# Attention scores on halves of TensorE's rows, in one layer of a hybrid encoder

## The chip, the cores and the metric

The kernel is one program on one core of a Trainium2 chip. The metric is the device time of one execution in microseconds, lower is better. The core has five engines that run their own instruction streams: TensorE (PE, with its weight loads shown apart as PEld), VectorE (DVE), ScalarE (ACT), GpSimd (POOL) and SyncE (SP), whose queue here does nothing but start transfers.

## What is computed

The layer normalises 1024 tokens and 16 meta tokens of width 1024, multiplies them by one wide input matrix, and feeds two branches: a neighbourhood attention over a token grid 64 wide and 16 high, and a gated linear recurrence in both directions. Both are gated, added, projected back, and followed by a feed-forward block with squared ReLU and a last norm. The change is in the attention branch:

```python
q_na, k_na, v_na = ...            # 8 heads of 64, for 16 meta and 1024 grid tokens
s_win  = einsum('brchd,brjwhd->bhrcjw', qg, k_blk) * scale   # 8 rows of keys for each query
s_win  = where(in_win, s_win + bias, -1e30)                  # window 16 wide in columns
s_meta = einsum('brchd,bmhd->bhrcm', qg, km) * scale
p      = softmax(concatenate([s_win, s_meta]))
o_grid = p_win @ v_blk + p_meta @ vm
```

All inputs and outputs are float32. The kernel keeps that accuracy by splitting a float32 number into a high part in TensorE's faster type (fp32r) and a low part, the remainder, and by adding three products: high by high, high by low, low by high.

## The kernel before, in words

The attention runs between the recurrence and the gates. The grid is cut into 8 strips of 8 columns by 16 rows, so a strip is 128 tokens, one tile of 128 partitions. A query in strip s sees keys in strips s-1, s and s+1 and the 16 meta keys; each strip of keys has 128 + 16 columns (SW = 144), so scores are 432 wide, or 288 in the first and the last strip. Two heads of 64 make a pair, there are four pairs (line 547), and each pair does this:

- It projects queries, keys and values (`proj`, lines 564, 582, 590): 24 matmuls for every 512 tokens, through the lines 135 to 137. What leaves PSUM is split into high and low by ACT and DVE. Queries go to `QX`, one tile per head: 64 partitions hold the high part, the other 64 the low part. Keys go to `KS`, the high part twice, and to `KL`, the low part in 64 partitions and zeros in the other 64. That takes four ACT and two DVE instructions for a piece of keys, two and two for a piece of queries (lines 558 to 581).
- `scores(s, i)` for strip s and head i (lines 605 to 623): two matmuls over all 128 rows, QX by KS (high times high plus low times high) and QX by KL (high times low), into one PSUM bank `nsc`, of which there are two. DVE adds the bias and takes the minimum (line 618; the signs are turned), ACT takes the exponential and the sum (620), DVE scales by the reciprocal (621, 622).
- `values(s, i)` (lines 625 to 663): three or four transposes of the probabilities on TensorE (633, 635) into `ppt`, the split into the tiles `PT` (ACT 644, DVE 645), and after each fourth strip the products with the values (649 to 658) into `pov`, added up by DVE (660, 662).

Heads are taken one after the other for four strips each (line 665), scores run two steps ahead of values, and `PT` has one pair of buffers, laid out by distance of key strip and query strip.

The order of instructions on each engine is made by a scheduler when the program is built, and each engine then keeps it. It fills TensorE with the next pair's projections while a pair's softmax runs, and in the last pair with the first products of the gates (`first_gates`, line 715, through the lines 691 to 693). These need the weight blocks that SP loads (line 123) and ACT and DVE split (125, 126). The gates also need four operands made by POOL during the attention (lines 228 to 246), which `second_operand` (739 to 745) loads again into the tile `gv`, of which there are five, and splits.

## Time and profile before

| | us |
|---|---|
| median of three runs | 1549.21 |
| lowest and highest run | 1549.18, 1552.02 |
| the profiled execution | 1550.2 |
| its span on the core | 1548.4 |
| TensorE busy in the span | 1502.1 |
| VectorE busy | 1008.4 |
| ScalarE busy | 654.7 |

A row of a timeline gives the start, the duration, the engine, the source line, what it writes and reads, its shape, and in brackets the idle time of the engine before it with what ended that. TensorE's matmuls follow each other before the one ahead has come to its end, so what one costs is read from the distance of two starts, not from its duration. Where a row stands for several instructions (x2) its start is that of the first.

### The profile page before, as it was taken

To read this page: it belongs to the slowest core of one execution; us is meant where nothing else is said; L and a number is where in the kernel's file an instruction comes from. 1 tells how busy PE (TensorE), PEld (TensorE's weight loads), DVE (VectorE), ACT (ScalarE), POOL (GpSimd) and SP (SyncE) were. 2 spreads that over 40 slices of the span, in tenths; PEclk is the share of its full clock that TensorE was granted. 3 is DMA by queue.
4 is the path that set the end of the run, shared out by engine and by line. 5 is a ranking of instruction groups with operands and counts; after the bars stand their busy time and mean duration, and the time that the engine had idled before them with its cause. 6 is when DMAs were issued, how large, how long until landed. Compare 5 with 4: busy or idle time off the path is not lost.

```text
span 1548.4 us, 23448 instructions
## 1 busy us (share of the span) xinstructions
PE 1502.1 (97%) x9188; PEld 1253.5 (81%) x9188; DVE 1008.4 (65%) x1592; ACT 654.7 (42%) x1168; POOL 401.8 (26%) x359
## 2 busy tenths in 40 slices
PE   6999999999999998999999999999999999999998
PEld 5788888878888887888888887888888788887886
DVE  6666666664876877666475369666666444879566
ACT  6231313124665666334122245555555433434444
POOL 4413131315315310011000032444444200237033
PEclk9999999999999999999999999999999999999999
DMA  5101010113123128434951324444444576563224
GB/s 181 43 28 56 28 56 28 55 29 128 49 72 119 55 69 272 136 123 163 339 178 41 109 91 148 165 155 153 153 150 148 169 273 233 190 231 107 98 82 150
DMA packets 142335, 195.61 MB, mean 126 GB/s; under 512 B 8064, under 2 KB 90112, under 8 KB 142224
## 3 DMA queue, kind: packets, MB, share of 16 engines
q1 hardware_dynamic: 133856, 173.40, 33.8%
q10 hardware_dynamic: 6192, 13.37, 2.2%
q0 software_dynamic: 2176, 7.34, 1.3%
q8 instruction: 72, 1.18, 0.3%
q14 instruction: 39, 0.32, 0.1%
HBM read 139.55 MB, written 54.53 MB: 125 GB/s over the span
## 4 chain that ended last, share of the span: by engine, by line
PE 83%; DVE 9%; issue 3%; ACT 2%; DMA 2%; POOL 1%; DVEq 0%; POOLq 0%; SPq 0%; ACTq 0%
PE mm L135 11%; PE mm L136 10%; PE mm L137 10%; PE mm L1112 4%; PE pa L1112 4%; PE pb L691 4%; PE pb L692 4%; PE pb L693 4%; PE pc L1112 4%; PE pb L1112 4%; PE pc L693 2%; PE pc L692 2%; PE pc L691 2%; PE pa L692 2%; PE pa L691 2%
## 5 line engine op out<-in xcount | busy, mean ns | idle before, releaser
L135 PE MATMUL mm<-aT,hi 128*128 128x512 f32 (+2 forms) x640 | 230.2, 360 | 2.7 <-DVE QX L563 1.5
L137 PE MATMUL mm<-aT,lo 128*128 128x512 f32 (+2 forms) x640 | 227.8, 356 | 0.0
L136 PE MATMUL mm<-aT,hi 128*128 128x512 f32 (+2 forms) x640 | 226.6, 354 | 0.0
L97 DVE TENSOR_TENSOR dl<-ur,dh 128x1024 fp32r<-128x1024 f32 x55 | 76.6, 1393 | 93.7 <-ACT dh L96 93.5
L135 PEld LDWEIGHTS mm<-aT,hi 128*128 128x128 f32 x640 | 121.9, 191 | 17.2 <-issue 1.7
L137 PEld LDWEIGHTS mm<-aT,lo 128*128 128x128 f32 x640 | 121.8, 190 | 13.5 <-POOL lo L126 0.3
L136 PEld LDWEIGHTS mm<-aT,hi 128*128 128x128 f32 x640 | 121.9, 190 | 12.4
L96 ACT CAST dh<-ur 128x1024 fp32r<-128x1024 f32 x55 | 57.9, 1053 | 162.5 <-issue 78.1
L125 ACT CAST hi<-raw 128x1024 fp32r<-128x1024 f32 x36 | 37.8, 1051 | 106.7 <-PE mm L136 75.6
L974 ACT CAST wh<-sx 128x512 fp32r<-128x512 f32 x70 | 42.5, 618 | 94.7 <-DMA sx<-in_w_up 33.1
L975 DVE TENSOR_TENSOR wl<-sx,wh 128x512 fp32r<-128x512 f32 x70 | 51.2, 738 | 31.0 <-ACT wh L974 31.0
L975 DVE TENSOR_TENSOR wl<-raw,wh 128x512 fp32r<-128x512 f32 x46 | 50.2, 1090 | 23.7 <-ACT wh L974 22.9
L979 ACT ACTIVATE uv<-uv 128x512 f32<-128x512 f32 x48 | 30.4, 632 | 67.4 <-DVE uv L1090 50.0
L1095 POOL TENSOR_TENSOR us<-u,uv 128x512 f32<-128x512 f32 x15 | 24.0, 1603 | 133.4 <-ACT uv L980 133.4
L1202 POOL TENSOR_TENSOR w<-w,tt 128x512 f32<-128x512 f32 x16 | 23.3, 1458 | 134.0 <-DVE tt L1201 120.4
L399 POOL TENSOR_TENSOR Y<-X,TN 128x512 f32<-128x512 f32 x20 | 35.0, 1749 | 86.1 <-DVE X L396 86.1
L691 PE MATMUL pb<-nt,wh 128*128 128x512 f32 x128 | 50.4, 394 | 3.6 <-DVE uv L1083 2.6
L126 DVE TENSOR_TENSOR lo<-raw,hi 128x1024 fp32r<-128x1024 f32 x34 | 43.2, 1270 | 15.6 <-ACT hi L125 15.4
L92 POOL TENSOR_SCALAR rtm<-ssq 128x1 f32<-128x1 f32 (+1 forms) x17 | 6.4, 376 | 180.4 <-ACT junk L924 156.0
L618 DVE CUSTOM_DVE_ANT_0 pr<-nsc,NB 128x432 f32<-128x432 f32 (+1 forms) x64 | 35.2, 559 | 26.6 <-PE nsc L613 26.5
L1112 PE MATMUL mm<-dl,dh 128*128 128x512 f32 x126 | 49.9, 396 | 2.1 <-DVE dl L97 2.1
L135 PE MATMUL mm<-o,hi 128*128 128x512 f32 x128 | 50.0, 390 | 0.6 <-DVE mix L850 0.6
(380 smaller groups left out, 4409.3 us busy)
## 6 DMA issues: line engine op xcount, KB each, us to landing
raw<-in_w_in SPq DMA_DIRECT2D x56, 512.0 KB, 3.9
ur<-usp SPq DMA_DIRECT2D x55, 512.0 KB, 3.5
raw<-in_w_up SPq DMA_DIRECT2D x16, 1024.0 KB, 5.5
usp<-us SPq DMA_DIRECT2D x60, 256.0 KB, 2.0
sg<-gsp SPq DMA_DIRECT2D x16, 512.0 KB, 4.3
w<-in_w_dn SPq DMA_DIRECT2D x16, 512.0 KB, 4.5
usp<-uv SPq DMA_DIRECT2D x30, 256.0 KB, 2.2
gsp<-gv ACTq DMA_DIRECT2D x24, 256.0 KB, 2.4
```

Of the source, the lines that this page charges most:

```text
L96: act.copy(hi, src)
L97: dve.tensor_tensor(lo, src, hi.bitcast(F32), op=ALU.subtract)
L126: eng.tensor_tensor(lo[:, :kc], raw[:, :kc], hi[:, :kc].bitcast(F32), op=ALU.subtract)
L135: pe.matmul(ps, lh, rh, start=first, stop=False)
L136: pe.matmul(ps, lh, rl, start=False, stop=False)
L137: pe.matmul(ps, ll, rh, start=False, stop=last)
L691: pe.matmul(ps, lhs[0][:, c], rhs[0][:, k], start=first and k == 0, stop=False, skip_group_check=True)
L692: pe.matmul(ps, lhs[0][:, c], rhs[1][:, k], start=False, stop=False, skip_group_check=True)
L693: pe.matmul(ps, lhs[1][:, c], rhs[0][:, k], start=False, stop=k == 3, skip_group_check=True)
L974: act.copy(v(hi), src)
L975: dve.tensor_tensor(v(lo), src, v(hi).bitcast(F32), op=ALU.subtract)
L1112: pe.matmul(ps, a[n == 2][:, q, j * P:(j + 1) * P], b[n == 1][:, q], start=first and n == 0, stop=last and n == 2, skip_group_check=True)
```

## The change

It touches four things.

1. Queries and keys are split into tiles of their own, `QH`, `QL`, `KH`, `KL`, with the two heads in the two halves of the partitions, by one ACT and one DVE instruction for each piece of both heads. The zeros in `KL` go.
2. `scores(s)` does both heads of a strip. Each head's 64 rows of TensorE are a tile of their own (`tile_position`), and three products of 64 rows (high by high, low by high, high by low) take the place of two of 128. The two heads' scores stand in the two banks of one PSUM tile, of which there is one where there were two of one bank.
3. Heads alternate within a strip, scores run one strip ahead, and the split probabilities lie four blocks to a query strip, in a pair of buffers for each head; the products with the values read them with a stride of three blocks.
4. The operands of the gates are loaded straight into the low tile and split in place; the results of the gates get five buffers of their own, in another pool.

The core of the diff ("..." for lines left out):

```diff
-    psum_pools(mx=1, s=2, t=2, b=1)
+    psum_pools(mx=1, s=1, t=2, b=1)
...
-        QX = [npl.tile([P, 8, P], F32R, name=f"QX{i}") for i in range(2)]
-        KS = [npl.tile([P, 8, SW], F32R, name=f"KS{i}") for i in range(2)]
-        KL = [npl.tile([P, 8, SW], F32R, name=f"KL{i}") for i in range(2)]
+        QH, QL = (npl.tile([P, 8, P], F32R, name=f"Q{v}") for v in "HL")
+        KH, KL = (npl.tile([P, 8, SW], F32R, name=f"K{v}") for v in "HL")
...
+        def ev_split(hi, lo):
+            def ev(ps, t0, n):
+                split(strips(hi, t0, n), strips(lo, t0, n), grid(ps))
+            return ev
...
-            def ev_q(ps, t0, n):
-                for i in range(2):
-                    b = 64 * i
-                    hi = strips(QX[i], b, t0, n)
-                    act.copy(hi, grid(ps, b))
-                    dve.tensor_tensor(strips(QX[i], 64 - b, t0, n), grid(ps, b), hi.bitcast(F32), op=ALU.subtract)
-            proj(C_QN + p * P, ev_q)
...
+            proj(C_QN + p * P, ev_split(QH, QL))
...
+            proj(C_KN + p * P, ev_split(KH, KL), mev_k)
...
-                sc = bank("s", "nsc").rearrange("p a b -> p (a b)")
-                ksl = KS[i][:, js[0]:js[-1] + 1].rearrange("p s c -> p (s c)")
-                kll = KL[i][:, js[0]:js[-1] + 1].rearrange("p s c -> p (s c)")
-                pe.matmul(sc[:, :w], QX[i][:, s], ksl, start=True, stop=False)
-                pe.matmul(sc[:, :w], QX[i][:, s], kll, start=False, stop=True)
+                sc = banks["s"].tile([P, 2, TH], F32, tag="s", name="nsc")
+                scs = [sc[:, i, :w] for i in range(2)]
+                for n, (q, k) in enumerate(((QH, KH), (QL, KH), (QH, KL))):
+                    for i in range(2):
+                        r = slice(64 * i, 64 * i + 64)
+                        pe.matmul(scs[i], q[r, s], k[r, js[0]:js[-1] + 1].rearrange("p s c -> p (s c)"),
+                                  start=n == 0, stop=n == 2, tile_position=(64 * i, 0))
...
-                    po[i] = [npr.tile([P, 22, P], F32R, tag=f"PT{q}", name=f"PT{q}") for q in range(2)]
...
-                        b = 3 * a + e0 + 3
-                        pe.matmul(ov[:, e0:e0 + ne], V[:, j, i], PH[:, b:b + ne], start=False, stop=False)
+                        b = slice(3 * e0 + a + 1, 3 * (e0 + ne - 1) + a + 2, 3)
+                        pe.matmul(ov[:, e0:e0 + ne], V[:, j, i], PH[:, b], start=False, stop=False)
...
-            steps = [(4 * g + e, i) for g in range(2) for i in range(2) for e in range(4)]
...
+            for s in [*range(8), None]:
+                if s is not None:
+                    if s % 4 == 0:
+                        PT = [[npr.tile([P, 16, P], F32R, tag=f"PT{i}{q}", name=f"PT{i}{q}") for q in range(2)]
+                              for i in range(2)]
+                    pend.append((s, *scores(s), PT))
+                if len(pend) > 1 or s is None:
+                    s_, js, prs, pts = pend.pop(0)
+                    for i in range(2):
+                        values(s_, i, js, prs[i], pts[i])
...
-            t = g_tile("gv", TH, bufs=5)
...
-            sp.dma_start(t, tsp[v][k])
-            split(aV[v][0][:, k], aV[v][1][:, k], t)
+            hi, lo = (t[:, k] for t in aV[v])
+            sp.dma_start(lo.bitcast(F32), tsp[v][k])
+            split(hi, lo, lo.bitcast(F32))
```

What the scheduler makes of it shows in the order of the instructions. On PE, where the first pair's attention begins, there stood before (nsc is the bank of scores, mm a projection, vpt the transposed values):

```order
L612 MATMUL nsc<-KS_3940,QX_3938 128x288
L613 MATMUL nsc<-KL_3942,QX_3938 128x288
L612 MATMUL nsc<-KS_3940,QX_3938 128x432
L613 MATMUL nsc<-KL_3942,QX_3938 128x432
L135 MATMUL mm<-aT_90,hi 128x512
L136 MATMUL mm<-aT_91,hi 128x512
L612 MATMUL nsc<-KS_3940,QX_3938 128x432
L613 MATMUL nsc<-KL_3942,QX_3938 128x432
```

At the same place there stands now:

```order
L595 MATMUL nsc<-KH,QH 128x288 x2
L595 MATMUL nsc<-KH,QL 128x288 x2
L595 MATMUL nsc<-KL,QH 128x288 x2
L135 MATMUL mm<-aT_90,hi 128x512
L136 MATMUL mm<-aT_91,hi 128x512
L137 MATMUL mm<-aT_90,lo 128x512
L576 MATMUL vpt<-ident,vT 128x128 x8
```

Six products of 64 rows for both heads of a strip stand where two strips of one head had two of 128 rows each. Further on in the same pair one such six is cut in two by products with the values (ppt are transposed probabilities, pov the products with the values):

```order
L617 MATMUL ppt<-ident,pr 128x128 x2
L619 MATMUL ppt<-ident,pr 128x128
L595 MATMUL nsc<-KH,QH 128x432 x2
L636 MATMUL pov<-PT_4228,Vn 64x384
L635 MATMUL pov<-PT_4227,Vn 128x256
L636 MATMUL pov<-PT_4228,Vn 64x256
L635 MATMUL pov<-PT_4227,Vn 128x128
L636 MATMUL pov<-PT_4228,Vn 64x128
L637 MATMUL pov<-PT_4228,Vn 128x512
L595 MATMUL nsc<-KH,QL 128x432 x2
L595 MATMUL nsc<-KL,QH 128x432 x2
```

This happens once in each pair, so the 32 strips make 36 unbroken runs of score products. On SP, where the last pair's attention runs, the loads of the gates' operands (from tsp) stood among the weight blocks (raw) like this:

```order
L123 DMA raw<-in_w_in 128x8x128
L765 DMA raw<-in_w_in 128x8x128
L744 DMA gv<-tsp_t_0_370 128x512
L744 DMA gv<-tsp_t_1_371 128x512
L744 DMA gv<-tsp_t_2_372 128x512
L744 DMA gv<-tsp_t_3_373 128x512
L744 DMA gv<-tsp_t_0_366 128x512
L123 DMA raw<-in_w_in 128x8x128
```

Now the first four, into aT, stand further ahead, and the second operand's go into the tile at:

```order
L726 DMA aT_93<-tsp_t_3_373 128x512
L123 DMA raw<-in_w_in 128x8x128
L747 DMA raw<-in_w_in 128x8x128 x3
L123 DMA raw<-in_w_in 128x8x128 x2
L726 DMA at_6887<-tsp_t_0_366 128x512
L726 DMA at_6887<-tsp_t_1_367 128x512
L726 DMA at_6887<-tsp_t_2_368 128x512
L123 DMA raw<-in_w_in 128x8x128
```

The tile at lies in the memory of the attention's right-hand pool, so its loads start when the last pair's attention has let go of it, and the last weight blocks of the first gates stand behind them.

More of the change, by code (lines that the diff above doesn't have):

```diff
@@ L525, in layer, with strips, grid @@
     gfp = gfs.enter_context(tc.tile_pool(name="gfp", bufs=1, side="right", reuse_waits="tile"))
-    psum_pools(mx=1, s=2, t=2, b=1)
+    psum_pools(mx=1, s=1, t=2, b=1)
     with (tc.tile_pool(name="npr", bufs=1, side="right", reuse_waits="tile") as npr,
           tc.tile_pool(name="np", bufs=1, reuse_waits="tile") as npl):
-        QX = [npl.tile([P, 8, P], F32R, name=f"QX{i}") for i in range(2)]
-        KS = [npl.tile([P, 8, SW], F32R, name=f"KS{i}") for i in range(2)]
-        KL = [npl.tile([P, 8, SW], F32R, name=f"KL{i}") for i in range(2)]
+        QH, QL = (npl.tile([P, 8, P], F32R, name=f"Q{v}") for v in "HL")
+        KH, KL = (npl.tile([P, 8, SW], F32R, name=f"K{v}") for v in "HL")
         vT = npl.tile([P, 9, P], F32, name="vT")
         V = npr.tile([P, 9, 2, P], F32R, name="Vn")
-        pool.memset(KL[0][64:128].bitcast(F32), 0.0)
-        pool.memset(KL[1][0:64].bitcast(F32), 0.0)
         pool.memset(vT[:, 8], 0.0)
-        def strips(t, p0, t0, n, w=None):
-            a = t[p0:p0 + 64, 0:8, t0 // 8:(t0 + n) // 8]
-            return a.rearrange("p s (r c) -> p s r c", c=8)
-        def grid(ps, p0):
-            return ps[p0:p0 + 64].rearrange("p (r s c) -> p s r c", s=8, c=8)
+        def strips(t, t0, n):
+            return t[:, 0:8, t0 // 8:(t0 + n) // 8].rearrange("p s (r c) -> p s r c", c=8)
+        def grid(ps):
+            return ps.rearrange("p (r s c) -> p s r c", s=8, c=8)
+        def ev_split(hi, lo):
+            def ev(ps, t0, n):
+                split(strips(hi, t0, n), strips(lo, t0, n), grid(ps))
+            return ev
         for p in range(NPAIR):
@@ L556, in layer @@
                                        op=ALU.subtract)
-            def ev_q(ps, t0, n):
-                for i in range(2):
-                    b = 64 * i
-                    hi = strips(QX[i], b, t0, n)
-                    act.copy(hi, grid(ps, b))
-                    dve.tensor_tensor(strips(QX[i], 64 - b, t0, n), grid(ps, b), hi.bitcast(F32), op=ALU.subtract)
-            proj(C_QN + p * P, ev_q)
-            def ev_k(ps, t0, n):
-                for i in range(2):
-                    b = 64 * i
-                    hi = strips(KS[i], b, t0, n)
-                    act.copy(hi, grid(ps, b))
-                    act.copy(strips(KS[i], 64 - b, t0, n), grid(ps, b))
-                    dve.tensor_tensor(strips(KL[i], b, t0, n), grid(ps, b), hi.bitcast(F32), op=ALU.subtract)
-            def mev_k(ps):
-                for i in range(2):
-                    b = 64 * i
-                    m = ps[b:b + 64].unsqueeze(1).broadcast_to([64, 8, NM])
-                    hi = KS[i][b:b + 64, :, P:]
-                    act.copy(hi, m)
-                    act.copy(KS[i][64 - b:128 - b, :, P:], m)
-                    dve.tensor_tensor(KL[i][b:b + 64, :, P:], m, hi.bitcast(F32), op=ALU.subtract)
-            proj(C_KN + p * P, ev_k, mev_k)
+            proj(C_QN + p * P, ev_split(QH, QL))
+            def mev_k(ps):
+                split(KH[:, :, P:], KL[:, :, P:], ps.unsqueeze(1).broadcast_to([P, 8, NM]))
+            proj(C_KN + p * P, ev_split(KH, KL), mev_k)
             def ev_vn(ps, t0, n):
-                for i in range(2):
-                    act.copy(strips(vT, 64 * i, t0, n), grid(ps, 64 * i))
+                act.copy(strips(vT, t0, n), grid(ps))
             def mev_vn(ps):
@@ L600, in layer, with scores @@
             block_sums(p, lambda: npl.tile([P, TH], F32, tag="bs", name="rt", bufs=3))
-            po = {}
             OT = npr.tile([P, T], F32, tag="OT", name="OT")
-            def scores(s, i):
+            def scores(s):
                 js = [j for j in (s - 1, s, s + 1) if 0 <= j < 8]
@@ L608, in scores @@
                 o = 432 if s == 0 else 720 if s == 7 else 0
-                sc = bank("s", "nsc").rearrange("p a b -> p (a b)")
-                ksl = KS[i][:, js[0]:js[-1] + 1].rearrange("p s c -> p (s c)")
-                kll = KL[i][:, js[0]:js[-1] + 1].rearrange("p s c -> p (s c)")
-                pe.matmul(sc[:, :w], QX[i][:, s], ksl, start=True, stop=False)
-                pe.matmul(sc[:, :w], QX[i][:, s], kll, start=False, stop=True)
-                pr = npr.tile([P, 432], F32, tag="pr", name="pr", bufs=5)
@@ L615, in scores @@
-                mn = npr.tile([P, 1], F32, tag="mn", name="mn", bufs=4)
-                sm = npr.tile([P, 1], F32, tag="sm", name="sm", bufs=4)
-                rc = npr.tile([P, 1], F32, tag="rc", name="rc", bufs=4)
-                dve.tensor_tensor_reduce(out=pr[:, :w], in0=sc[:, :w], in1=NB[:, i, o:o + w], scale=1.0,
-                                         scalar=3.0e38, op0=ALU.add, op1=ALU.min, accum_out=mn)
-                act.activation(pr[:, :w], pr[:, :w], AF.Exp, bias=mn, scale=-1.0, accum_out=sm)
@@ L621, in scores @@
-                dve.reciprocal(rc, sm)
-                dve.tensor_scalar(pr[:, :w], pr[:, :w], rc, None, op0=ALU.mult)
-                return js, pr
-            def values(s, i, js, pr):
+                sc = banks["s"].tile([P, 2, TH], F32, tag="s", name="nsc")
[5 more added lines that the diff above has]
+                                  start=n == 0, stop=n == 2, tile_position=(64 * i, 0))
@@ new lines, in scores @@
+                prs = []
+                for i in range(2):
+                    pr = npr.tile([P, 432], F32, tag="pr", name="pr", bufs=6)
+                    mn = npr.tile([P, 1], F32, tag="mn", name="mn", bufs=4)
+                    sm = npr.tile([P, 1], F32, tag="sm", name="sm", bufs=4)
+                    rc = npr.tile([P, 1], F32, tag="rc", name="rc", bufs=4)
+                    dve.tensor_tensor_reduce(out=pr[:, :w], in0=scs[i], in1=NB[:, i, o:o + w], scale=1.0,
+                                             scalar=3.0e38, op0=ALU.add, op1=ALU.min, accum_out=mn)
+                    act.activation(pr[:, :w], pr[:, :w], AF.Exp, bias=mn, scale=-1.0, accum_out=sm)
+                    dve.reciprocal(rc, sm)
+                    dve.tensor_scalar(pr[:, :w], pr[:, :w], rc, None, op0=ALU.mult)
+                    prs.append(pr)
@@ L626, in values @@
+                return js, prs
+            def values(s, i, js, pr, PT):
                 g, e = divmod(s, 4)
-                if e == 0:
-                    po[i] = [npr.tile([P, 22, P], F32R, tag=f"PT{q}", name=f"PT{q}") for q in range(2)]
-                PH, PL = po[i]
+                PH, PL = PT
                 m = len(js)
@@ L635, in values @@
                 pe.transpose(pt[:, m], pr[:, cen * SW + NM:cen * SW + NM + P], ident)
-                b0 = 3 * (js[0] - 4 * g) + e + 3
-                if s < 7:
-                    runs = [(0, m + 1, b0)]
-                else:
-                    runs = [(0, m, b0), (m, 1, 4 * e + 9)]
-                for k, n, b in runs:
-                    hi = PH[:, b:b + 3 * n - 2:3]
-                    act.copy(hi, pt[:, k:k + n])
-                    dve.tensor_tensor(PL[:, b:b + 3 * n - 2:3], pt[:, k:k + n], hi.bitcast(F32), op=ALU.subtract)
+                k0 = 4 * e + js[0] - s + 1
+                for k, n, b in [(0, m + 1, k0)] if s < 7 else [(0, m, k0), (m, 1, 4 * e + 3)]:
+                    split(PH[:, b:b + n], PL[:, b:b + n], pt[:, k:k + n])
                 if e < 3:
@@ L648, in values @@
                 ov = bank("b", "pov")
-                pe.matmul(ov, V[:, 8, i], PH[:, 9:22:4], start=True, stop=False)
+                pe.matmul(ov, V[:, 8, i], PH[:, 3::4], start=True, stop=False)
                 for a in range(-1, 5):
@@ L654, in values @@
                         e0, ne = es[0], len(es)
-                        b = 3 * a + e0 + 3
-                        pe.matmul(ov[:, e0:e0 + ne], V[:, j, i], PH[:, b:b + ne], start=False, stop=False)
-                        pe.matmul(ov[:64, e0:e0 + ne], V[:, j, i, :64], PL[:, b:b + ne], start=False, stop=False)
-                pe.matmul(ov, V[:, 8, i], PL[:, 9:22:4], start=False, stop=True)
+                        b = slice(3 * e0 + a + 1, 3 * (e0 + ne - 1) + a + 2, 3)
+                        pe.matmul(ov[:, e0:e0 + ne], V[:, j, i], PH[:, b], start=False, stop=False)
+                        pe.matmul(ov[:64, e0:e0 + ne], V[:, j, i, :64], PL[:, b], start=False, stop=False)
+                pe.matmul(ov, V[:, 8, i], PL[:, 3::4], start=False, stop=True)
                 low = npr.tile([64, 4, P], F32, tag="low", name="low")
@@ L663, in values @@
                                   low.rearrange("p s (r c) -> p s r c", c=8), op=ALU.add)
-            steps = [(4 * g + e, i) for g in range(2) for i in range(2) for e in range(4)]
             pend = []
-            for st in steps:
-                pend.append((*st, *scores(*st)))
-                if len(pend) > 2:
-                    values(*pend.pop(0))
-            for st in pend:
-                values(*st)
+            for s in [*range(8), None]:
[6 more added lines that the diff above has]
+                    s_, js, prs, pts = pend.pop(0)
+                    for i in range(2):
+                        values(s_, i, js, prs[i], pts[i])
             pool.dma_start(osp[1][p], OT)
@@ L782, in gate_pair @@
         chain(pb, W["s2"], aV["t2"], True)
-        u1, u3, u2 = (g_tile("gv", TH, bufs=5) for _ in range(3))
+        u1, u3, u2 = (gpr.tile([P, TH], F32, tag="gu", name="gu", bufs=5) for _ in range(3))
         dve.tensor_tensor(u1, pb, g1[m], op=ALU.add)
```

## The prediction

> **What bounds the kernel now.** I read the busy time of the engines on the page first, then the table of engines by stretches of the attention, then TensorE's waits in it. The page's first rows give the engine:

> ```profile
> PE 1502.1 (97%) x9188; PEld 1253.5 (81%) x9188; DVE 1008.4 (65%) x1592; ACT 654.7 (42%) x1168; POOL 401.8 (26%) x359
> ```

> The stretches give each engine's busy time in 20 us (PE, PEld, DVE, ACT, POOL, then granted clock, DMA share, GB/s):

> ```profile
> 440.00:460.00 20.00, 19.97 (x122) 16.82 (x122) 19.03 (x58) 14.62 (x38) 0.00 (x0) 1.00 0.10 27
> ...
> 580.00:600.00 20.00, 17.57 (x92) 14.29 (x91) 16.39 (x31) 14.91 (x29) 0.54 (x1) 1.00 0.77 249
> 600.00:620.00 20.00, 18.01 (x78) 14.31 (x77) 11.72 (x16) 12.58 (x22) 0.00 (x0) 1.00 0.86 277
> ```

> TensorE is full inside the attention (19.97 of 20) at a granted clock of 1.00, and loses time only at its end. VectorE stands close behind it (19.03). What TensorE waited for between 355 and 625 us (total, times, longest):

> ```profile
> PE ppt L633 <- DVE PT L645: 2.4, 1, 2.4
> PE mm L135 <- DVE QX L563: 1.5, 1, 1.5
> PE mm L691 <- ACT hi L125: 1.5, 1, 1.5
> PE ppt L633 <- DVE pr L622: 1.4, 3, 0.5
> PE mm L135 <- DVE KL L572: 1.2, 2, 0.6
> PE mm L693 <- DVE lo L126: 0.5, 1, 0.5
> ```

> That is 8.5 us in all. So a saving on ACT or DVE can bring 8.5 us at the very most, and the change is otherwise worth what it is worth on TensorE's own stream.

> **The change part by part.** *The score products.* The tile view counts them (durations in ns, min/median/max):

> ```profile
> L612 PE MATMUL nsc<-KS,QX x64: 292/379/469, 381.2 to 578.0; 128*128 128x432 f32 x48, 128*128 128x288 f32 x16
> L613 PE MATMUL nsc<-KL,QX x64: 291/356/366, 381.3 to 578.1; 128*128 128x432 f32 x48, 128*128 128x288 f32 x16
> ```

> The durations overlap, so the price is the distance of starts:

> ```profile
> 442.46 0.37 PE L612 MATMUL nsc<-KS,QX 128*128 128x432 f32 x1
> 442.46 0.19 PEld L613 LDWEIGHTS nsc<-KL,QX 128*128 128x128 f32 x1
> 442.66 0.35 PE L613 MATMUL nsc<-KL,QX 128*128 128x432 f32 x1
> 442.85 0.40 PE L136 MATMUL mm<-aT,hi 128*128 128x512 f32 x1
> ...
> 578.01 0.29 PE L612 MATMUL nsc<-KS,QX 128*128 128x288 f32 x1
> 578.14 0.30 PE L613 MATMUL nsc<-KL,QX 128*128 128x288 f32 x1
> 578.28 0.39 PE L692 MATMUL mm<-aT,hi 128*128 128x512 f32 x1
> ```

> A 432-wide product takes 0.195 us of the stream (442.46 to 442.85 for two), a 288-wide one 0.135 (578.01 to 578.28 for two). Now: 96 x 0.195 + 32 x 0.135 = 23.0 us. After: 24 strips of three pairs of 432 and 8 of three pairs of 288. If a pair, one product in each half of the rows, runs in the time of one: 72 x 0.195 + 24 x 0.135 = 17.3 us, so **-5.8** (before rounding). That halves of the array run side by side is seen here for halves of the columns only, in line 390:

> ```profile
> 96.49 1.15 PE L390 MATMUL sc<-QQ,X 128*64 128x64 f32 x32
> 97.57 0.50 PE L135 MATMUL mm<-aT,hi 128*128 128x512 f32 x1
> ```

> From the first of the 32 to the next line's product are 97.57 - 96.49 = 1.08 us, 34 ns each with all of the switching, where a full product of 128 columns takes 0.11 us (next fence), so an estimated 55 ns for half its width. I take rows to do the same; the case that they don't is a rival.

> *Going in and out of the tiles.* The program has one place with products on part of the rows, line 446 (16 rows), among full ones; the first row is the tile's own (ns), the rest its timeline:

> ```profile
> L462 PE MATMUL pu<-V,KT x112: 270/275/377, 111.3 to 342.3; 128*128 128x128 f32 x112
> ...
> 188.27 0.48 PE L135 MATMUL mm<-aT,hi 128*128 128x512 f32 x1
> 188.68 0.48 PE L446 MATMUL pum<-Vm,kmT 16*128 16x128 f32 x2
> 189.09 0.49 PE L462 MATMUL pu<-V,KT 128*128 128x128 f32 x2
> 189.34 0.48 PE L136 MATMUL mm<-aT,hi 128*128 128x512 f32 x1
> 189.66 0.38 PE L462 MATMUL pu<-V,KT 128*128 128x128 f32 x2
> 189.79 0.47 PE L137 MATMUL mm<-aT,lo 128*128 128x512 f32 x1
> ```

> Two of line 462 last 0.38 from the first's start to the second's end (189.66) where one lasts 0.275: 0.11 apart. The same neighbours without line 446 are the comparison. From the 512-wide product to line 446 it is 0.41, to line 462 0.32: +0.09 for going in. Line 446's two, as wide, take 0.41 to the next start, at 0.11 each 0.22: +0.19. The two of line 462 behind it take 0.25, the later two 0.13: +0.11 for having come out. Together 0.39 us for one run of row tiles. I charge it to each of the 36 unbroken runs that the order gives: **+14.0**. Some 0.09 of it may be a load that the longer products here hide, so the lower end is 36 x 0.30 = 10.8; the lowest, nothing, is a rival, because narrowing the columns costs nothing:

> ```profile
> 448.97 0.28 PE L656 MATMUL pov<-PT,Vn 128*128 128x256 f32 x1
> 449.08 0.28 PE L657 MATMUL pov<-PT,Vn 128*64 128x256 f32 x1
> 449.20 0.34 PE L656 MATMUL pov<-PT,Vn 128*128 128x384 f32 x1
> ```

> Here 0.11 to 0.12 is what 256 columns stream in either shape. I take the 0.39 since line 446 is the only one that, as the scores will, changes the rows. [...]

> *The splits.* Between 340 and 640 us:

> ```profile
> L562 ACT CAST QX<-mm 64x512 fp32r<-64x512 f32 x16 | 9.2, 580 | 1.6 <-DVE QX L563 1.0 <-PE pov L658 0.3 <-PE pov L657 0.2
> L563 DVE TENSOR_TENSOR QX<-mm,QX 64x512 fp32r<-64x512 f32 x16 | 10.9, 688 | 0.8 <-ACT QX L562 0.3
> L571 ACT CAST KS<-mm 64x512 fp32r<-64x512 f32 x8 | 4.6, 581 | 0.1
> ```

> An instruction on 64 partitions is taken to cost what one on 128 does. A piece of queries then falls from two ACT and two DVE instructions to one and one, a piece of keys from four and two to one and one. Where nothing else is queued, the projection's bank comes free 0.69 us earlier for queries (0.58 + 2 x 0.69 against 0.58 + 0.69) and 1.2 for keys (second high part after the copy: 3 x 0.58 + 0.69 = 2.4 against 1.3). Of the waits above that takes 0.7 of the 1.5 for QX and the whole 1.2 for KL: **-1.9**. All else that ACT and DVE save lies beside a full TensorE and counts nothing; the two memsets on POOL and the strided reads of the probabilities (the meta products already read with a stride of four blocks) I put at nothing, with POOL idle in the first row above as their cover.

> *Order of heads, buffers, gates.* Line 633 waits 1.4 for pr; scores run one strip ahead instead of two steps, the same distance, and TensorE comes 0.39 later each time by the switches, so I count 1.2 saved. The 2.4 for PT is the last pair's tail; now products of the gates stand between those transposes: 1.5 saved. Loading into the tile frees five buffers early, but the second operand's loads must wait for the attention's memory and stand ahead of weight blocks. Seven loads of 0.26 MB and two blocks of 0.52 are 2.9 MB, at the 277 GB/s of the last stretch 10.4 us. By the order, 82 products of the gates (144 columns add 0.06 above, so 512 take 0.228) run between the last product with values and the first that needs the last of these blocks, 18.7 us: hidden. If that cover were gone, 10 us would show. Ahead of the last product with values stand 62 of the gates' products where there were 72, so ten more are left to cover the 2.0 of hi and lo: half of that, 1.0, saved. Together **-3.7**; at the lower end nothing.

> Sum: -5.8 + 14.0 - 1.9 - 3.7 = **+2.6 us**. The profiled execution took 1550.2, 1.0 above the median of 1549.2; from it the sum gives 1552.8, and against the median **1551.8**. Its own bounds: -5.8 + 10.8 - 8.5 = -3.5, and -5.8 + 14.0 - 1.9 = +6.3.

> **The rivals.**

> *Row halves cost no switch* (lines 656 and 657 are the rule, and line 446 is slow for its 16 rows). Then -5.8 - 1.9 = -7.7 at best. But VectorE has 0.97 us of air in 20, so some comes back as its wait; with half of 5.8 given back, -4.8: 1544.4. Against it: line 446 behaves so at all four places where it stands.

> *The halves run one after the other.* 144 x 0.195 + 48 x 0.135 = 34.6 us, +11.6 in place of -5.8: 11.6 + 14.0 - 5.6 = +20.0: 1569.2. For it: no row of before shows two row tiles at once. Against it: line 390.

> *The single score tile makes TensorE wait* (the other side). Before, one bank was free for each score; now a tile holds both heads and there is one, so a strip's products start only after both of the last strip's reductions:

> ```profile
> L618 DVE CUSTOM_DVE_ANT_0 pr<-nsc,NB 128x432 f32<-128x432 f32 (+1 forms) x64 | 35.2, 559 | 26.6 <-PE nsc L613 26.5
> ```

> Two take 1.1 us, in a VectorE queue that is nearly full. The scheduler puts projections and values between strips; where these run short TensorE stands. If half of one reduction, 0.28 us, shows in all 28 later strips, it is 7.8, in half of them 3.9: +6.5 to +10.4, in the middle 1557.7. It decides if VectorE lies more than the work between two strips behind. Against it: VectorE has half of line 563's 10.9 us less to do over the attention.

> *Loads aren't hidden.* In each run two of the three load pairs would stand open, 0.10 each as in line 446: 36 x 0.20 = +7.2, so +9.8: 1559.0. Against it: 442.46, where line 613's load starts with line 612's product on the same 128 rows. [...]

> **How the numbers follow.** Chances: the forecast 0.60, free switches 0.15, halves in turn 0.08, the single tile 0.13, open loads 0.04. The measurement tells 0.2%, 3.1 us, from no change. Within the forecast's own range (1545.7 to 1555.5) I give 0.05 to faster by more than that, 0.35 to within, 0.20 to slower. Free switches add 0.15 to faster; the other three add 0.25 to slower. So 0.20, 0.35, 0.45. The range takes in the free switches with all kept, 1549.2 - 7.7 = 1541.5, and the single tile's upper end, 1559.6, and leaves out the halves in turn and the forecast's tails: 1541 to 1560.

> **What would show it.** In the changed kernel's timeline: line 595's two heads start a few ns apart and pairs 0.195 apart (if 0.39, halves run in turn); the start before a run and behind it lie some 0.2 further apart than streaming says (if not, switches are free); load rows of the second pair start with the first pair's products (if after, loads are open). Among the waits, the one for QX halves and the one for KL is gone; a new one of line 595 for the reduction means the single tile. The forecast is wrong if TensorE's idle time in the attention grows, or the runs cost under 0.2 or over 0.5 us each.

## The result and the profile after

| | before | after |
|---|---|---|
| median | 1549.20 us (4 runs, 1548.41 to 1552.02) | 1559.87 us (4 runs, 1559.21 to 1561.03) |
| profiled execution, span | 1548.4 | 1557.4 |
| ratio | | 1.0066, 95% interval 1.0049 to 1.0084 |

The changed kernel is slower by 0.66%, 10 us (7.6 to 13 by the interval). Nearly all of it lies in one stage. The next fences give it for both kernels, from the recurrence's last transposes (line 495) to the last product of the first gates (line 693, now 675): length, then busy time of PE, PEld, DVE, ACT, POOL, granted clock, DMA share, GB/s. Before:

```profile
353.17:623.42 270.25, 261.53 (x1526) 222.25 (x1524) 194.59 (x464) 167.50 (x375) 77.96 (x78) 1.00 0.34 109
```

After:

```profile
352.45:631.42 278.97, 270.75 (x1589) 217.62 (x1588) 180.19 (x440) 138.40 (x307) 73.81 (x76) 0.99 0.33 105
```

The stage is 8.7 us longer, of 9.0 between the two spans. VectorE lost 14 us of work and ScalarE 29, and it brought nothing: TensorE is the engine that is busy. This stage is what the experiments are read by below, since the whole varies (the kernel before had medians of 1549.2 to 1551.4 beside the different experiments). Each length is that of one execution, and it holds that execution's stretches of half clock on TensorE, which last 3.41 us each (last section) and cost up to half of that, 1.7 us. The kernel before had none in its stage, the changed kernel two in a row. The run zero_rows, whose TensorE does the same work in the same order in this stage, had three and took 280.7 us instead of 279.0. So differences under 2 us between two stages show nothing unless their clock is looked at.

TensorE's waits between 355 and 632 us in the changed kernel (total, times, longest):

```profile
PE ppt L617 <- DVE PT L97: 3.0, 5, 2.0
PE pov L628 <- ACT PT L96: 1.5, 1, 1.5
PE mm L673 <- ACT hi L125: 1.2, 1, 1.2
PE vpt L576 <- ACT vT L567: 0.8, 1, 0.8
PE mm L675 <- DVE lo L126: 0.5, 1, 0.5
PE ppt L617 <- DVE pr L607: 0.4, 2, 0.2
PE ppt L617 <- DVE rc L606: 0.3, 2, 0.2
```

The waits for the split queries and keys are gone, and line 595 does not appear: TensorE waits in no place for the single tile of scores. But the sum is 7.7 us where it was 8.5. The last run of score products, in the timeline:

```profile
580.81 0.39 PE L673 MATMUL mm<-aT,hi 128*128 128x512 f32 x1
581.12 0.40 PE L595 MATMUL nsc<-KH,QH 64*128 64x288 f32 x2
581.36 0.29 PE L595 MATMUL nsc<-KH,QL 64*128 64x288 f32 x2
581.49 0.29 PE L595 MATMUL nsc<-KL,QH 64*128 64x288 f32 x2
581.71 0.50 PE L674 MATMUL mm<-aT,hi 128*128 128x512 f32 x1
582.05 0.39 PE L675 MATMUL mm<-aT,lo 128*128 128x512 f32 x1
```

Each row of line 595 holds both heads, and pairs follow each other at 0.13 us, so the halves run side by side. Going in costs 0.31 - 0.23 = 0.08, the second pair comes 0.24 after the first instead of 0.135 (+0.105), going out is 0.22 (+0.085), and the next product is late by 0.34 - 0.23 = 0.11: 0.38 us for the run, where 0.39 was forecast. By the same count the other 288-wide runs between 512-wide products lie at 0.38 to 0.39.

The last pair's tail is the new part. TensorE there:

```profile
585.02 0.39 PE L675 MATMUL mm<-aT,lo 128*128 128x512 f32 x1
587.45 0.44 PE L617 MATMUL ppt<-ident,pr 128*128 128x128 f32 x2 [2.04 <-DVE PT L97]
...
590.13 0.80 PE L628 MATMUL pov<-PT,Vn 128*128 128x512 f32 x1 [1.53 <-ACT PT L96]
...
593.60 0.63 PE L673 MATMUL mm<-aT,hi 128*128 128x512 f32 x1
...
596.15 0.40 PE L675 MATMUL mm<-aT,lo 128*128 128x512 f32 x1
```

The clock that it was granted (third column from the right):

```profile
585.00:590.00 5.00, 1.51 (x8) 0.62 (x6) 4.07 (x10) 4.75 (x12) 0.00 (x0) 0.93 0.48 157
590.00:595.00 5.00, 4.87 (x16) 4.20 (x17) 4.00 (x8) 3.18 (x5) 0.00 (x0) 0.50 0.53 164
```

TensorE was busy for 1.5 us of the first 5, and its granted clock was 0.50 from 589.30 to 596.13. The twelve products with the values took 593.60 - 590.13 = 3.47 us; before, the first head's same twelve took 1.92, by these two rows (the first of them, and what follows the last):

```profile
583.61 0.50 PE L649 MATMUL pov<-PT,Vn 128*128 128x512 f32 x1
...
585.53 0.49 PE L633 MATMUL ppt<-ident,pr 128*128 128x128 f32 x3
```

The six products behind took 2.55 instead of 6 x 0.228 = 1.37. Half the clock thus cost 1.55 + 1.18 = 2.7 us. The second head's twelve took 1.80 at full clock (597.99 to 599.79), as in the kernel before (1.81, from 592.05), so it is the clock and not the new stride of their reads. What TensorE waited for stands on ScalarE:

```profile
581.84 1.28 ACT L694 ACT_TABLE_LOAD   x1
583.13 0.60 ACT L694 ACTIVATE go<-mm 128x512 f32<-128x512 f32 x1
583.75 1.28 ACT L605 ACT_TABLE_LOAD   x1
585.05 0.54 ACT L605 ACTIVATE pr<-pr,mn 128x288 f32<-128x288 f32 x1
```

The first gates' sigmoid stands between the exponentials of the last two strips with a table load of 1.28 us on each side, 3.2 us in which the softmax stands still; the next copies into PT, which the transposes wait for, stand behind that, at 586.10. The kernel before loaded the same tables in its tail (577.39, 579.30 and 583.57). But there the first head's last products with the values ran at 583.61 already (above), and 32 of the gates' products lay between the last scores and the last product with values, by the trace; now both heads hang on the last strip, and there are 25.

### The profile page after: what moved, and what is told of

Its sections match the earlier page's. It is cut to its first block, busy times and chain, and to the rows that moved or that the text cites. A ratio compares the mean times of both kernels' runs of the same rounds, so it can differ in the third digit from the quotient of the medians.

```text
span 1557.4 us, 23476 instructions
## 1 busy us (share of the span) xinstructions
PE 1511.5 (97%) x9252; PEld 1248.7 (80%) x9252; DVE 996.9 (64%) x1568; ACT 626.1 (40%) x1100; POOL 396.7 (25%) x357
## 4 chain that ended last, share of the span: by engine, by line
PE 81%; DVE 9%; issue 3%; ACT 2%; DMA 2%; POOL 1%; SPq 0%; DVEq 0%; ACTq 0%; POOLq 0%
PE mm L135 11%; PE mm L136 10%; PE mm L137 10%; PE mm L1094 4%; PE pa L1094 4%; PE pb L673 4%; PE pb L674 4%; PE pb L675 4%; PE pc L1094 4%; PE pb L1094 4%; PE pc L674 2%; PE pc L675 2%; PE pc L673 2%; PE pa L674 2%; PE pa L675 2%
## 5 line engine op out<-in xcount | busy, mean ns | idle before, releaser
L135 PE MATMUL mm<-aT,hi 128*128 128x512 f32 (+2 forms) x640 | 230.9, 361 | 0.0
L137 PE MATMUL mm<-aT,lo 128*128 128x512 f32 (+2 forms) x640 | 227.7, 356 | 0.0
L136 PE MATMUL mm<-aT,hi 128*128 128x512 f32 (+2 forms) x640 | 226.0, 353 | 0.0
L135 PEld LDWEIGHTS mm<-aT,hi 128*128 128x128 f32 x640 | 121.6, 190 | 15.5 <-issue 1.7
L137 PEld LDWEIGHTS mm<-aT,lo 128*128 128x128 f32 x640 | 121.6, 190 | 13.8 <-issue 0.2
L136 PEld LDWEIGHTS mm<-aT,hi 128*128 128x128 f32 x640 | 121.8, 190 | 12.9
L125 ACT CAST hi<-raw 128x1024 fp32r<-128x1024 f32 x36 | 37.7, 1050 | 105.2 <-PE mm L136 78.7
L126 DVE TENSOR_TENSOR lo<-raw,hi 128x1024 fp32r<-128x1024 f32 x34 | 41.8, 1229 | 23.4 <-ACT hi L125 23.3
L603 DVE CUSTOM_DVE_ANT_0 pr<-nsc,NB 128x432 f32<-128x432 f32 (+1 forms) x64 | 34.5, 564 | 26.7 <-issue 26.4
L135 PE MATMUL mm<-o,hi 128*128 128x512 f32 x128 | 49.9, 390 | 0.5 <-DVE mix L832 0.5
```

Source lines behind the costliest of these rows:

```text
L126: eng.tensor_tensor(lo[:, :kc], raw[:, :kc], hi[:, :kc].bitcast(F32), op=ALU.subtract)
L135: pe.matmul(ps, lh, rh, start=first, stop=False)
L136: pe.matmul(ps, lh, rl, start=False, stop=False)
L137: pe.matmul(ps, ll, rh, start=False, stop=last)
```

## The experiments

Besides the time, each is read by the stage row defined above. Ratios are to the kernel before, with their 95% intervals.

### Full rows again, interleaved heads kept

```diff
-        QH, QL = (npl.tile([P, 8, P], F32R, name=f"Q{v}") for v in "HL")
-        KH, KL = (npl.tile([P, 8, SW], F32R, name=f"K{v}") for v in "HL")
+        QX = [npl.tile([P, 8, P], F32R, name=f"QX{i}") for i in range(2)]
+        KS = [npl.tile([P, 8, SW], F32R, name=f"KS{i}") for i in range(2)]
+        KL = [npl.tile([P, 8, SW], F32R, name=f"KL{i}") for i in range(2)]
...
-                for n, (q, k) in enumerate(((QH, KH), (QL, KH), (QH, KL))):
-                    for i in range(2):
-                        r = slice(64 * i, 64 * i + 64)
-                        pe.matmul(scs[i], q[r, s], k[r, js[0]:js[-1] + 1].rearrange("p s c -> p (s c)"),
-                                  start=n == 0, stop=n == 2, tile_position=(64 * i, 0))
+                for i in range(2):
+                    for n, k in enumerate((KS, KL)):
+                        pe.matmul(scs[i], QX[i][:, s], k[i][:, js[0]:js[-1] + 1].rearrange("p s c -> p (s c)"),
+                                  start=n == 0, stop=n == 1)
```

The splits are those of the kernel before again. To make room, four of the eight g1 tiles are allocated behind the attention.

> Only the row halves and the tiles that feed them are undone; interleaved heads, two-bank score tile, packed probabilities and the gates' operands stay as in the changed kernel. Theory (row switches cost 14.0 us against 5.3 us of streaming saved, and the rest of the loss is the last pair's tail): 1559.9 - 14.0 + 5.3 = 1551.2, plus 0 to 2 us for the slower splits of queries and keys, so 1551 to 1553, with TensorE still idle over 3 us around the last transposes. Rival (the tail comes from the row switches, which make TensorE late): 1546 to 1549, with no such idle time. Second rival (the switches cost little in the end and the interleaving is the loss): over 1556.

Measured: 1555.58 us, ratio 1.0029 (1.0019 to 1.0038). The stage, and TensorE's largest waits:

```profile
354.45:629.60 275.15, 262.24 (x1526) 222.93 (x1524) 193.83 (x463) 164.27 (x365) 77.80 (x78) 1.00 0.33 107
```

```profile
PE pov L654 <- DVE OT L667: 4.1, 7, 1.4
PE ppt L643 <- DVE PT L97: 3.1, 7, 0.9
PE mm L135 <- DVE QX L571: 2.0, 4, 1.5
```

As a time, 4.2 us above the 1551.36 of the kernel before beside it, this is just over what the theory allows (1551 to 1553 against 1549.2); the second rival asked for more. As an account the theory missed: taking out the row tiles gave back 3.8 us of the stage, not 8.7, and the interleaving that is left costs 4.9 against the kernel before. No idle time of 3 us is left around the last transposes (the longest waits there are 1.2 and 0.8). The clock stayed at 1.00, so 2.7 of the 3.8 us are the half clock of the changed kernel. In place of the switches stand waits for VectorE, most of all for OT: both heads' products with the values come together, there is one bank for them, and the second head waits until VectorE has cleared it. The same kernel ran once more, for its stage alone; its label, full_two_banks, promises a change that it does not have:

> The kernel with full rows and interleaved heads once more, one look for the trace alone: its stage from the end of the recurrence to the last of the first gates took 275.2 us where the kernel before took 270.3. Theory (a steady price of interleaving): 274 to 277 again. Rival (a mishap of one execution): 270 to 272.

It took 1552.23 us in one run, and the stage 274.3, again without half clock: a steady price, 4 to 5 us over the kernel before.

### The sigmoid without its table

```diff
-        act.activation(t, src, AF.Sigmoid)
+        if c < 8 and h == 0 and c % 2 == 0 and src is not t:
+            act.activation(t, src, AF.Tanh, scale=0.5)
+            pool.tensor_scalar(t, t, 0.5, 0.5, op0=ALU.mult, op1=ALU.add)
+            pool.dma_start(gsp[c][:, h * TH:(h + 1) * TH], t)
+        else:
+            act.activation(t, src, AF.Sigmoid)
...
```

> The changed kernel, with the sigmoid of the four gate tiles that fall into the last pair's softmax taken as 0.5 tanh(x/2) + 0.5 (tanh on ScalarE, the rest and the store on GpSimd), so that ScalarE needs no table load there. Theory (two loads of 1.28 us stand between the exponentials of the last two strips, TensorE starves behind them and its clock falls to half): 2 to 3 us of idle time and the 2.9 us of half clock go, 1554 to 1556, clock 1.00 throughout. Rival (both heads' last values come together and TensorE has nothing else in its order, tables or not): 1558 to 1560, clock still at 0.5 there.

> The kernel before with the same four gate tiles by tanh. Theory: its one wait of 2.4 us in the tail shrinks, 1547 to 1549.2. Rival (the table loads lie beside a busy TensorE in both kernels): 1549.2, no change, and then the loads are no cause of the difference either.

In the changed kernel: 1554.70 us, ratio 1.0014 (1.0006 to 1.0023). In the kernel before: 1552.40, ratio 1.0011 (1.0000 to 1.0023). The stage and the largest waits of the changed kernel with tanh:

```profile
352.77:628.05 275.28, 268.86 (x1589) 216.75 (x1588) 179.41 (x438) 135.71 (x305) 80.67 (x84) 0.99 0.33 107
```

```profile
PE mm L673 <- ACT go L699: 1.9, 1, 1.9
PE pov L628 <- DVE OT L641: 1.9, 1, 1.9
```

And of the kernel before with tanh:

```profile
352.77:624.51 271.74, 262.95 (x1525) 223.09 (x1524) 195.06 (x464) 165.25 (x373) 82.49 (x86) 0.99 0.34 108
```

```profile
PE mm L691 <- ACT hi L125: 2.8, 1, 2.8
PE mm L693 <- DVE lo L126: 2.0, 2, 1.5
PE ppt L633 <- DVE PT L645: 0.7, 1, 0.7
```

The same edit takes 3.7 us from the changed kernel's stage and gives the kernel before 1.5 more. In the kernel before, the wait for PT falls from 2.4 to 0.7 as well, but TensorE only comes earlier to gate weights that are not there yet (hi and lo 4.8 where they were 2.0). Its waits add up to 8.6 us where they were 8.5, and the 1.5 us more are a stretch of half clock behind the wait for hi (612.78 to 616.19). So only in the changed order did taking the table loads away save time. By its time the theory for the changed kernel held (1554 to 1556); the one for the kernel before did not, since that got no faster. That half clock would go was wrong as well: one stretch of it, where there were two, came behind the new wait for OT (last section).

### The gates' operands as before

```diff
-            hi, lo = (t[:, k] for t in aV[v])
-            sp.dma_start(lo.bitcast(F32), tsp[v][k])
-            split(hi, lo, lo.bitcast(F32))
+            t = g_tile("gv", TH, bufs=5)
+            sp.dma_start(t, tsp[v][k])
+            split(aV[v][0][:, k], aV[v][1][:, k], t)
...
-        u1, u3, u2 = (gpr.tile([P, TH], F32, tag="gu", name="gu", bufs=5) for _ in range(3))
+        u1, u3, u2 = (g_tile("gv", TH, bufs=5) for _ in range(3))
```

> The changed kernel with its fourth part undone (the gates' operands through the five buffers again). Theory (these loads are hidden): within 1 us of 1559.9. Rival (they push the gates' products out of the tail, which then has nothing to fill it): 1554 to 1557, with more of the gates' products ahead of the last product with values and a clock of 1.00.

1563.91 us, ratio 1.0079 (1.0067 to 1.0091), which overlaps the changed kernel's interval. The stage took 278.89 us, the changed kernel's 278.97: in the attention and its tail this part is worth nothing, as forecast, and the rival falls. The time alone would not show it: it is 4 us over the 1559.9 of the theory, 1.9 when each is taken against the kernel before beside it.

### Two strips in one run

```diff
-    psum_pools(mx=1, s=1, t=2, b=1)
+    psum_pools(s=1, t=1, b=1)
...
+                big = banks["s"].tile([P, 4, TH], F32, tag="s", name="nsc")
+                with tc.high_priority():
+                    for s, js, w, o, scs in todo:
...
```

Here todo holds two strips; four of the g1 tiles are moved as above, the transposes and the projections have a bank less each, and the scheduler puts the scores first.

> The changed kernel with the scores of two strips issued in one run of row tiles, into one four-bank tile of scores (which leaves one bank for the transposes and none for the third projection buffer): 20 unbroken runs in place of 36. Theory (each run of row tiles costs TensorE 0.39 us on its way in and out): 16 x 0.39 = 6.2 us less of such time, 1553 to 1555 in all, less what TensorE newly waits for with fewer banks. Rival (the switches lie in time in which TensorE would wait for VectorE anyway, so that fewer of them only bring the waits back): the distances around the runs shrink by the same 6 us, the waits grow by it, and the time stays within 2 us of the changed kernel.

1584.30 us, ratio 1.0215 (1.0193 to 1.0237); the stage took 305.9. Its waits:

```profile
PE mm L135 <- DVE QL L97: 8.6, 4, 2.9
...
PE nsc L598 <- DVE mn L608: 3.1, 6, 1.1
```

The time tells nothing about the price of a switch, and both the theory and its rival missed: the waits that came with the fewer banks and the new order were worth more than all switches, and 27 us of half clock came with them. The wait of nsc for VectorE's reductions, absent from the changed kernel, is here.

### Two banks for the products with the values

```diff
-    psum_pools(mx=1, s=1, t=2, b=1)
+    psum_pools(s=1, t=2, b=2)
```

> The changed kernel with two banks for the products with the values in place of one (the third projection buffer is given up for it). Theory (interleaving brings both heads' products with the values at once, and the second head's must wait for VectorE to clear the one bank): in the tail the two heads' products run without a gap between them, the wait for OT is gone, 0.5 to 2 us off, the half clock perhaps too; 1555 to 1559. Rival (the third projection buffer was worth as much): 1560 to 1563.

> The same with the sigmoid of all eight first gate tiles by tanh, so that no table load stands ahead of the last product of the first gates. Theory (table loads and the single bank are what the tail loses, row switches the rest): 2 us under the kernel with tanh alone, 1552 to 1553 beside a kernel before of 1549 to 1551, with no stretch of half clock. Rival (the tail is bound by the chain from the last scores over ScalarE and VectorE itself): no better than tanh alone, 1554 to 1556.

1560.94 us, ratio 1.0065 (1.0047 to 1.0083), and with tanh for all eight tiles 1562.44, ratio 1.0076 (1.0056 to 1.0097). The first one's waits:

```profile
PE mm L135 <- DVE KL L97: 3.2, 3, 1.3
PE mm L135 <- DVE QL L97: 2.9, 1, 2.9
```

No OT, and the clock is 1.00 in every stretch of the tail, but the projections wait 6.1 us for their splits with a buffer less. The rival was right for the first. For the second, theory and rival (1554 to 1556) were both wrong: without the third buffer tanh has nothing to win (stage 280.3 and 282.0, the latter with a stretch of half clock at the start of the attention).

### The price of a switch by itself

```diff
-                        mm3(pm, hi[:, c], lo[:, c], sh, sl, k == 0, k == 3)
+                        mm3(pm, hi[:, c], lo[:, c], sh, sl, k == 0, False)
+                        pe.matmul(pm, zero[:64], sh[:64], start=False, stop=k == 3, tile_position=(0, 0))
```

> The changed kernel with 128 further products in the stage behind the gates (the branch projections, where TensorE is full): each adds 64 rows of zeros, 512 columns wide, in the lower half of the rows, to a sum that is on its way, so it goes into row tiles and out again 128 times and changes no value. Streaming alone is 128 x 0.228 = 29 us. Theory (going in costs 0.09 and having come out 0.2, as in the score runs, whose third 0.1 is the second pair's load): 128 x (0.228 + 0.30) = 68 us more than the changed kernel, 1627 us. Rival (a switch costs nothing where the stream is full, and the distances around the score runs are waits of another kind): 29 us more, 1589.

1639.62 us, ratio 1.0572 (1.0558 to 1.0586); against the changed kernel 1550.8 x (1.0572 - 1.0066) = 78 us more. In its timeline:

```profile
799.82 0.40 PE L139 MATMUL mm<-o,lo 128*128 128x512 f32 x1
800.14 0.49 PE L833 MATMUL mm<-o,zero 64*128 64x512 f32 x1
800.57 0.50 PE L137 MATMUL mm<-o,hi 128*128 128x512 f32 x1
800.90 0.39 PE L138 MATMUL mm<-o,hi 128*128 128x512 f32 x1
...
801.46 0.49 PE L833 MATMUL mm<-o,zero 64*128 64x512 f32 x1
```

The period of four products is 801.46 - 800.14 = 1.32 us, and four times 0.228 are 0.91: 0.40 us for a visit to row tiles, and by the whole, (78 - 29) / 128 = 0.38. The theory, 0.30, was too low: the 0.1 that a run of six shows at its second pair appears here as a longer way out (0.43 where 0.228 is streaming). So in a full stream a visit costs 0.4 us, whether it holds one product or six. (No run added full-row products of zeros instead; that one product more costs only its 0.228 us is taken from the full-row products beside it.)

### VectorE's copy on ScalarE

```diff
-                dve.tensor_copy(low, ov[64:])
+                act.copy(low, ov[64:])
```

> The changed kernel with the copy that starts clearing the bank of the products with the values on ScalarE in place of VectorE (16 of 0.69 us). Theory (in the changed kernel TensorE, with its switches, is slower than VectorE, so VectorE has time to spare but in the tail): within 2 us of the changed kernel, 1557 to 1560. Rival (VectorE bounds the interleaved attention here too): 1552 to 1556.

> The kernel with full rows and interleaved heads, with the same copy on ScalarE. Theory (without the switches TensorE waits for VectorE, most of all for the one bank of the products with the values, 4 us for OT; that is where the other half of the switches' 8.7 us went): that wait falls by 2 to 4 us, 1551 to 1553 where the kernel before has 1551. Rival (interleaving costs by the order of its products, not by VectorE): no change, 1555 to 1556.

With row halves: 1557.01 us, ratio 1.0043 (1.0030 to 1.0055), stage 276.3. With full rows: 1552.52, ratio 1.0008 (0.9999 to 1.0017), and this stage:

```profile
350.72:622.57 271.85, 262.64 (x1525) 224.40 (x1524) 180.57 (x447) 173.67 (x381) 76.25 (x78) 0.99 0.33 108
```

Moving sixteen copies takes 2.4 to 3.3 us from the stage with full rows, and 2.7 from the one with row halves, where 1.5 of it is one stretch of half clock less. By its number that run is at the lower end of its theory, but it is 6.2 us slower than the kernel before beside it where the changed kernel was 10.7, so the copy was worth more than the theory's 2 us. With full rows no wait for OT is left in the list, as that theory said, and what the stage has over the 270.25 of the kernel before is no more than its one stretch of half clock (586.45 to 589.86). So VectorE's queue at that one bank was most of what interleaving costs. No run moved the copy in the kernel before, so what it would bring there is open.

### All of it with full rows

The edits of full_rows, tanh_after and low_on_act together:

```diff
-                dve.tensor_copy(low, ov[64:])
+                act.copy(low, ov[64:])
...
+            act.activation(t, src, AF.Tanh, scale=0.5)
```

> Full rows, interleaved heads, the copy that clears the bank on ScalarE, and the four gate tiles by tanh. Theory (what is left over the kernel before is the tail: a wait of 3.3 us for the split probabilities behind two table loads, and 1.7 us of half clock after it): 271.9 - 3 to 5 = 267 to 269 us for the stage from the end of the recurrence to the last of the first gates, where the kernel before took 270.3; so 1 to 3 us under the kernel before, ratio 0.998 to 0.9995. Rival (ScalarE, with the copies and the exponentials, now sets the tail): no change against the same kernel without tanh, ratio 1.000 to 1.002.

1550.72 us, ratio 0.9996 (0.9985 to 1.0008): no difference to the kernel before. The stage took 271.0 us, not 267 to 269. The tail's wait for PT is short, but this came:

```profile
PE mm L699 <- ACT go L725: 2.6, 1, 2.6
```

That is the next gates' sigmoid (line 725), the first left in this order, with a projection bank behind it; in the changed kernel a table load ahead of a sigmoid took 1.28 us. The wait for PT and the half clock behind it went, as the theory said, but not their time: the new wait brought a stretch of half clock of its own (611.88 to 615.29). So the rival's outcome, no clear change against the same kernel without tanh, is the one that came, though not by its reason. No version here beats the kernel before.

## Why the prediction was right or wrong

The measured 1559.87 lies at the upper edge of the range, 8 us above the forecast, on the side that had the larger chance. That it lies inside at all is luck: the forecast's own bounds ended at 1555.5, and the range went up to 1560 for the single tile of scores, which did not come. The forecast's own signs did not show the miss either: a run costs 0.38 us, within 0.2 to 0.5, and TensorE's idle time did not grow.

*Streaming, -5.8.* Held for what came: pairs run side by side at one product's price. The rival of halves in turn falls. What went was priced too low: added up over the trace, the 128 score products of the kernel before took 26.7 us from start to next start, not 23.0. The forecast read the 0.195 us at an undisturbed pair; where several pairs follow each other it is often more (starts at 382.30, 382.57, 382.80, 383.11 and 383.30). Why is not shown.

*Switches, +14.0.* Held: 0.38 to 0.40 per visit in the runs read above and in the kernel made for it, against 0.39. (Line 446 is not the only place with part of the rows, as the forecast said: line 111 has eight products of 16 rows at the start. The sum does not rest on it.) That they are free, as narrower columns are in the kernel before (256 columns take 0.11 us at 448.97 on the whole width and 0.12 at 449.08 on half of it), falls; so do the open loads, which would have made it 0.59.

*Splits, -1.9.* The waits for QX and KL are gone from the list, 2.7 us, and a new one for vT takes 0.8: 1.9. That this is the forecast's number is partly chance: it kept 0.8 of the wait for QX and knew of no wait for vT.

*Order of heads, buffers, gates, -3.7.* **This step failed.** It took 1.5 of the 2.4 us that TensorE waited for PT in the tail as saved, because the gates' products would stand between the last transposes. They do not: the idle time there is 2.0 + 1.5 us, and 2.7 of half clock came with it, 6.2 us where 2.4 were. That is 5.3 us of the error. The half clock had no term in the forecast at all. The 1.2 for pr was not saved either (pr, rc and the short waits for PT: 0.4 + 0.3 + 1.0 = 1.7, where pr was 1.4), and of the 1.0 for the gates' weights 0.3 (2.0 to 1.7).

Added up, -5.8 + 14.0 - 1.9 + 3.8 + 0.3 - 0.3 = +10.1 for a stage that grew by 8.7. The 1.4 us between them lie on the side of TensorE's stream: without waits and half clock it grew by 6.0 us (261.5 to 267.5, from the starts in the two traces), not by the 14.0 - 5.8 = 8.2 of the forecast, and the kernel before's dearer score products (above) account for that with some to spare.

*The single tile.* As written the rival did not come: line 595 waits for nothing. But its kind did, at another bank: the one for the products with the values. The forecast did not look at it since the products themselves were unchanged. Its price is hidden in the changed kernel, whose TensorE is slowed by the switches, and shows when they are taken out: 4 to 5 us, mostly given back by moving a copy from VectorE. Hence the two halves of the loss by experiment: interleaving 4 to 5 us, row halves another 4 to 6 on top, and not 8 for the row halves alone. The second half is measured twice: 3.8 us by the stages with the copy on VectorE (5.7 by the two ratios), of which 2.7 are half clock, and 4.4 with the copy on ScalarE (4.5 by the medians), where both stages have one stretch of it.

*What I can't settle:* how the loss divides between the two without their overlap, and whether fewer switches would help with banks to spare; no kernel here had them.

## What to carry to other kernels

Halves of the rows do run side by side here (pairs of 288 columns start 0.13 us apart), but each visit to half rows and back costs a full stream 0.38 to 0.40 us, so the runs must be long: six products of 0.135 to 0.195 us, in pairs, save 0.18 us by the forecast's prices (0.29 by the 26.7 us above) and pay 0.39. When the order of work changes, look at every buffer that the order fills, also those whose instructions the diff leaves alone, and read the last round by itself: there is nothing left to fill TensorE, and in the changed kernel waits of 2.0 and 1.5 us there came with 2.7 us more in clock.

## What the runs showed of the hardware

In the changed kernel with tanh, TensorE was idle for about 2 us in a stream that was otherwise full, and its granted clock was 0.50 from 596.11 on:

```profile
593.34 0.39 PE L673 MATMUL mm<-aT,hi 128*128 128x512 f32 x1
595.63 0.47 PE L628 MATMUL pov<-PT,Vn 128*128 128x512 f32 x1 [1.90 <-DVE OT L641]
```

At full clock a product would have started at 593.57 at the latest, so the gap is 2.1 us. The kernel before had a gap of 2.4 us in its tail with the clock at 1.00 throughout. So the length of the gap alone does not decide in these two.

In the kernel before and in the changed one, from 60 us on and but for the stretch that each program ends in, half clock lasts 3.41 us (from 68.26 before; from 67.06 and 971.59 after) or twice that (from 589.30 after). The three starts of the changed kernel lie 153 and 112 times 3.413 us apart. Cut into pieces of 3.41 us counted from such a start (596.11 with tanh), the two executions show their gaps like this, first the one with tanh:

```profile
592.70:596.11 3.41, 1.51 (x9) 0.99 (x7) 3.35 (x7) 1.53 (x2) 0.00 (x0) 1.00 0.15 56
596.11:599.52 3.41, 3.41 (x13) 2.93 (x12) 1.73 (x2) 0.00 (x0) 0.00 (x0) 0.50 0.53 153
```

And the kernel before:

```profile
583.67:587.09 3.42, 2.45 (x17) 2.00 (x16) 1.82 (x5) 3.21 (x5) 0.00 (x0) 1.00 1.06 365
587.09:590.50 3.41, 2.03 (x13) 1.82 (x14) 3.41 (x5) 2.45 (x6) 0.00 (x0) 1.00 0.79 305
```
